# Seven block products for eight in the gate and up products of four feed-forward layers

## The chip, the core and the metric

The kernel runs on one core of a Trainium2 chip. The core has a matrix engine (TensorE, PE in the profile), VectorE (DVE), ScalarE (ACT), GpSimd (POOL) and SyncE (SP), which here only issues DMAs. Each engine takes its instructions in the order in which they stand in its own queue. The metric is the device time of one execution in microseconds (us); lower is better.

## The reference

Two blocks of two layers each run over 512 tokens of 1024 features in float32. Each layer has a mixer (windowed attention with sinks in A, neighbourhood attention on a grid in B, a gated delta rule in C, windowed attention with 16 meta tokens in D; A and B also attend to 256 memory tokens) and then a feed-forward (FFN) with 2816 hidden features:

```python
# A, B (first block)
h = rmsnorm(x, norm_ffn[i])
gu = h @ w_gate_up[i]
x = x + (jax.nn.silu(gu[..., :D_FF]) * gu[..., D_FF:]) @ w_down[i]
...
# C, D (second block): a causal convolution of 3 taps over the tokens of the gate
gate, val = jnp.split(h @ w_up, 2, -1)
gate = causal_dwconv(gate, conv_w)
return (jax.nn.silu(gate) * val) @ w_down
```

In the second block 16 meta tokens stand ahead of the 512, so that C's FFN has 528 tokens and D's needs 512 and a few before them for the convolution.

## The kernel before

Everything lies transposed: 128 features on the partitions, tokens along the free axis, so the stream is 8 tiles X[k] of 128 x 512 (or 528). Every float32 product is made of three matmuls (`mm3`): both operands are split into a high and a low part (`split`: ACT copies the high part, DVE subtracts it from the operand for the low part), and hi*hi, hi*lo and lo*hi are added in a PSUM bank.

`ffn` walks over NFF = 22 tiles f of 128 gate and 128 up columns. For each f two weight pieces of 4 K chunks x 256 columns (128 of the gate, 128 of the up half) are loaded by SP (`wcols`, `wpiece`: three `raw` buffers, four pairs `hi`, `lo`), split, and multiplied with the 8 operand tiles xs (`linT`): 8 x 3 matmuls for the gate and 24 for the up product, each over up to 512 tokens, which fill one PSUM bank. 528 tokens are taken as two halves of 264, in D the gate as 258 + 256. The norm's scale rs (one value per token) is not in the operands: it multiplies the products when they leave PSUM (`scaled`). At f = 0 it is still to come: `Held` keeps the products, `nj.sums()` and `nj.rows()` make rs, then they are scaled. In C and D `conv` follows on the gate (one ACT instruction and two on DVE), then SiLU on ACT (L877), the product with the up half (`ut`, L883) and its split into `ah`, `al`.

The down product runs over GROUPS of 8, 8 and 6 tiles f: after each group, for 8 output tiles j, 3 matmuls per f of the group are added in a bank (24, 24 and 18), from pieces of 256 output columns. The results of the first two groups are added to the stream X[j] on DVE (`resid`, L573). Those of the last go to `done`: a function of the next stage that adds the stream and starts the next norm, tile by tile, in A with a transposition of the token grid (`to_cols`, L1035), then the operands `xh`, `xl` of the next layer (L393, L394) and the sum of squares (L428).

A scheduler sets the order of the instructions on each engine from the order in which the code emits them, their priorities and the buffers that are free (62 `slot` buffers of 128 x 544, five `wk` buffers, three PSUM banks `mm`, others by the names `s` and `o`). During the FFN of A, `mid` calls steps of `load_biases`: six tiles `TB` of layer B's relative biases, by 96 small DMAs on GpSimd's queue. Layer B's memory keys and values, made in layer A, stay in slots until B uses them.

## Time and profile before

| | us |
|---|---|
| median of 3 runs | 2553.48 |
| lowest, highest | 2551.66, 2554.62 |
| span of the profiled execution | 2552.4 |
| PE busy | 2520.9 (99%) |
| DVE busy | 1423.0 (56%) |
| ACT busy | 968.8 (38%) |
| GpSimd busy | 275.8 (11%) |

The profiled execution took 2552.4 us from its first instruction to its last, 1.1 us under the median. The FFN of A lies at about 236 to 603 us of the span, B's at 800 to 1187, C's at 1576 to 1960 and D's at 2178 to the end. A matmul's recorded duration overlaps that of the next one, so its price in a stream is the distance between two starts. The granted clock is a share of TensorE's full speed.

### The profile page before, as it was taken

How to read it: one execution, taken by the hardware profiler on the slowest of the kernel's cores; microseconds unless marked ns; L12 is line 12 of the kernel's file. 1: busy time of each engine (PE TensorE's matmuls, PEld its weight loads, DVE VectorE, ACT ScalarE, POOL GpSimd, SP SyncE). 2: the span in 40 equal slices, each digit the busy share in tenths (PEclk: the TensorE clock that was granted, in tenths of full speed). 3: DMA queues.
4: the chain of work that ended last, by engine and by line, in shares of the span. 5: the costliest groups of instructions: out<-in, count | busy, mean ns of one | idle time of the engine just before them, and what ended most of it. 6: DMA issues, size and time to landing. Idle time of an engine off the chain costs nothing.

```text
span 2552.4 us, 40552 instructions
## 1 busy us (share of the span) xinstructions
PE 2520.9 (99%) x16222; PEld 2203.4 (86%) x16222; DVE 1423.0 (56%) x2838; ACT 968.8 (38%) x1687; POOL 275.8 (11%) x451
## 2 busy tenths in 40 slices
...
DMA packets 333648, 224.80 MB, mean 88 GB/s; under 512 B 43939, under 2 KB 324948, under 8 KB 333460
## 3 DMA queue, kind: packets, MB, share of 16 engines
...
## 4 chain that ended last, share of the span: by engine, by line
PE 47%; DVE 2%; issue 1%; POOL 0%; ACT 0%; POOLq 0%; DVEq 0%; ACTq 0%
PE mm L253 13%; PE mm L254 13%; PE mm L255 13%; PE pso L1874 1%; PE pss L1454 1%; PE pss L1447 1%; PE pss L1859 1%; PE pss L1431 0%; PE pss L339 0%; PE pss L733 0%; PE pss L1433 0%; PE pso L1879 0%; PE pss L734 0%; DVE xt L1420 0%; PE pss L1854 0%
## 5 line engine op out<-in xcount | busy, mean ns | idle before, releaser
L253 PE MATMUL mm<-xh,hi 128*128 128x264 f32 (+3 forms) x2752 | 916.4, 333 | 7.6 <-ACT xh L393 3.2
L254 PE MATMUL mm<-xl,hi 128*128 128x264 f32 (+3 forms) x2752 | 907.7, 330 | 0.5 <-DVE xl L394 0.5
L255 PE MATMUL mm<-xh,lo 128*128 128x264 f32 (+3 forms) x2752 | 906.1, 329 | 0.0
L217 DVE TENSOR_TENSOR lo<-raw,hi 128x1024 fp32r<-128x1024 f32 (+1 forms) x386 | 464.6, 1204 | 344.8 <-ACT hi L216 342.4
L216 ACT ACTIVATE hi<-raw 128x1024 fp32r<-128x1024 f32 (+1 forms) x386 | 400.2, 1039 | 660.6 <-PE mm L254 579.8
L253 PEld LDWEIGHTS mm<-xh,hi 128*128 128x128 f32 x2752 | 523.2, 190 | 61.7 <-issue 7.5
L254 PEld LDWEIGHTS mm<-xl,hi 128*128 128x128 f32 x2752 | 523.5, 190 | 47.2 <-DVE xl L394 1.3
L255 PEld LDWEIGHTS mm<-xh,lo 128*128 128x128 f32 x2752 | 523.3, 190 | 47.5 <-issue 0.5
L254 PE MATMUL mm<-al,hi 128*128 128x512 f32 (+1 forms) x880 | 308.0, 350 | 0.1
L253 PE MATMUL mm<-ah,hi 128*128 128x512 f32 (+1 forms) x880 | 308.0, 350 | 0.0
L255 PE MATMUL mm<-ah,lo 128*128 128x512 f32 (+1 forms) x880 | 307.8, 350 | 0.0
L573 DVE TENSOR_TENSOR xr<-mm,xr 128x264 f32<-128x264 f32 (+1 forms) x168 | 90.5, 542 | 188.0 <-PE mm L255 187.9
L254 PEld LDWEIGHTS mm<-al,hi 128*128 128x128 f32 x880 | 165.5, 188 | 23.1 <-DVE al L315 0.3
L253 PEld LDWEIGHTS mm<-ah,hi 128*128 128x128 f32 x880 | 165.6, 188 | 22.8
L255 PEld LDWEIGHTS mm<-ah,lo 128*128 128x128 f32 x880 | 165.4, 188 | 22.6
L290 DVE TENSOR_TENSOR gt<-mm,rs 128x512 f32<-128x512 f32 (+3 forms) x128 | 66.3, 518 | 185.5 <-PE mm L255 184.4
L877 ACT ACTIVATE gt<-gt 128x512 f32<-128x512 f32 x44 | 27.8, 632 | 176.6 <-DVE gt L290 176.4
L314 ACT ACTIVATE ah<-ut 128x512 fp32r<-128x512 f32 (+1 forms) x88 | 56.0, 636 | 86.3 <-DVE ut L883 86.3
L846 ACT ACTIVATE cy<-gt,fwcol 128x528 f32<-128x528 f32 (+1 forms) x44 | 32.1, 731 | 147.9 <-DVE gt L290 145.5
L254 PE MATMUL mm<-ol,hi 128*128 128x512 f32 (+1 forms) x256 | 87.6, 344 | 0.0
L255 PE MATMUL mm<-oh,lo 128*128 128x512 f32 (+1 forms) x256 | 87.4, 343 | 0.0
L290 DVE TENSOR_TENSOR ut<-mm,rs 128x512 f32<-128x512 f32 (+1 forms) x108 | 63.7, 590 | 42.2 <-PE mm L255 40.5
...
## 6 DMA issues: line engine op xcount, KB each, us to landing
raw<-in_w_gate_up_dram SPq DMA_DIRECT2D x176, 256.0 KB, 3.2
raw<-in_ffn_w_up_dram SPq DMA_DIRECT2D x176, 256.0 KB, 3.4
...
```

What stands on the lines that cost most here:

```text
L216: A.activation(r32(hi[:, :nk, :w]), raw[:, :nk, :w], AF.Copy)
L217: V.tensor_tensor(r32(lo[:, :nk, :w]), raw[:, :nk, :w], hi[:, :nk, :w], ALU.subtract)
L253: PE.matmul(ps, r32(hi), r32(xh), start=first, stop=False)
L254: PE.matmul(ps, r32(hi), r32(xl), start=False, stop=False)
L255: PE.matmul(ps, r32(lo), r32(xh), start=False, stop=last)
L290: V.tensor_tensor(dst[:, o:o + n], ps[:, :n], rs[:, o:o + n], ALU.mult)
L314: A.activation(r32(dst_h), src, AF.Copy)
L573: V.tensor_tensor(X[j][:, o:o + n], ps[:, :n], X[j][:, o:o + n], ALU.add)
L846: A.activation(out[:, lo:T], src[:, lo:T], AF.Copy, scale=taps[-1])
L877: A.activation(gt[:, w], gt[:, w], AF.Silu)
L1447: PE.matmul(py[q, h], am[q, h], x[q, h], start=True, stop=True)
L1454: PE.matmul(pzt[q, h], y[q, h], xt[q, h], start=True, stop=True)
```

## The change

For f >= NPLAIN = 3 the gate and up products of a tile are computed by blocks. The weights of f are a 2 x 2 array of blocks (first and second half of K, by gate and up columns), the normed operands another (halves of K by halves of the tokens), and the four results (gate and up by halves of the tokens) come from seven block products in place of eight, with sums of blocks ahead of and behind them. `seven` loads the two raw pieces, makes three new sums and one in place on DVE (L302 to L305) and splits seven blocks into four pieces `hi`, `lo`. `Blocks` builds the seven operands of the tokens for each of 4 K chunks: from `normed` (L995, DVE: x times the norm's weight times rs) with three subtractions on GpSimd (L339, L352, L357) and splits between them; this stands behind f = 0 and f = 1. `blocks_to` runs the seven products of 12 matmuls each in the order 1, 5, 6, 7, 2, 4, 3, over half the tokens (256 in A and B, 264 in C, 258 in D), three copies out of PSUM on ACT (L378, L380, L389), four additions on DVE (L383, L386, L392, L394) and one on GpSimd (L387). Products 2 and 3 go on adding to the banks of 1 and 5. Since the operands are normed, these tiles need no scaling by rs.

The down product has groups of 4, 4, 4, 4, 4 and 2 tiles. Its output tiles are emitted between the gate and up tiles of the next group, two after each f (four in the last group of two), and those of the last group at the end. `resid` runs for five groups. The biases `TB` go through a DRAM copy by 16 DMAs and 6 loads on SP's queue, and layer B's memory keys and values are written to DRAM and loaded back as `memb` there. Comments are gone, so lines move: L217 is L424 in the changed kernel, L290 is L398, L573 is L682, L883 is L1047, L1035 is L1200, L394 is L503, L428 is L537.

```diff
-GROUPS = [(0, 8), (8, 8), (16, 6)]
+GROUPS = [(0, 4), (4, 4), (8, 4), (12, 4), (16, 4), (20, 2)]
...
-NSLOT = 62
+NSLOT = 60
 NWK = 5
-NRAW = 3
+NRAW = 4
 NHI = 4
+NQT = 3
+NPLAIN = 3
...
-TAGS = {'t': (3, ['PT'])}
+TAGS = {'t': (3, ['PT', 's1', 's2', 's4'])}
...
+    def seven(loads, nk):
+        r0, r1 = [wp.tile([P, 4, 256], F32, tag="raw", name=nm("raw"), bufs=NRAW) for _ in range(2)]
+        for r, ld in zip((r0, r1), loads):
+            for n0, nn, src in ld:
+                nc.sync.dma_start(r[:, :nk, n0:n0 + nn], src)
...
+        V.tensor_tensor(s1, r0[b_], r1[b_], ALU.add)
+        V.tensor_tensor(s2, s1, r0[a_], ALU.subtract)
+        V.tensor_tensor(r0[b_], r0[a_], r0[b_], ALU.subtract)
+        V.tensor_tensor(s4, r1[a_], s2, ALU.subtract)
+        res = {}
+        for keys, srcs in (((1, 5), (r0[a_], s1)), ((6, 7), (s2, r0[b_])), ((2, 4), (r1[:, :nk, :],)), ((3,), (s4,))):
+            h, l = [wp.tile([P, 4, 256], F32, tag=x, name=nm(x), bufs=NHI) for x in ("hi", "lo")]
+            for i, src in enumerate(srcs):
+                w = slice(i * P, i * P + src.shape[2])
+                split(h[:, :nk, w], l[:, :nk, w], src)
+            for i, key in enumerate(keys):
+                res[key] = [(h[:, k, i * P:(i + 1) * P], l[:, k, i * P:(i + 1) * P]) for k in range(nk)]
+        return res
+    class Blocks:
+        def __init__(self, nk, o, n, tag, eng):
+            self.n, self.o, self.tag, self.eng = n, o, tag, eng
+            self.ops = {i: [None] * nk for i in range(1, 8)}
+            self.raw = [None] * nk
...
+        def first(self, k, z):
+            h, l = slot(self.tag), slot(self.tag)
+            v = self.win(z)
+            split(self.part(h, 0), self.part(l, 0), v[:, 0, :])
+            self.eng.tensor_tensor(v[:, 0, :], v[:, 1, :], v[:, 0, :], ALU.subtract)
+            split(self.part(h, 1), self.part(l, 1), v[:, 0, :])
+            for i, key in enumerate((1, 5)):
+                self.ops[key][k] = self.part(h, i), self.part(l, i)
+            self.raw[k] = v
+        def second(self, k, z):
+            v, t = self.win(z), self.raw[k]
+            h, l = slot(self.tag), slot(self.tag)
+            split(self.both(h), self.both(l), v)
+            for i, key in enumerate((2, 3)):
+                self.ops[key][k] = self.part(h, i), self.part(l, i)
+            self.eng.tensor_tensor(t, v[:, 1, :].unsqueeze(1).to_broadcast([P, 2, self.n]), t, ALU.subtract)
+            h, l = slot(self.tag), slot(self.tag)
+            split(self.both(h), self.both(l), t)
+            for i, key in enumerate((6, 7)):
+                self.ops[key][k] = self.part(h, i), self.part(l, i)
+            self.eng.tensor_tensor(v[:, 0, :], v[:, 0, :], t[:, 0, :], ALU.subtract)
+            h = slot(self.tag)
+            split(self.part(h, 0), self.part(h, 1), v[:, 0, :])
+            self.ops[4][k] = self.part(h, 0), self.part(h, 1)
+    def product(ps, i, ws, bl, more=False):
+        w, b = ws[i], bl.ops[i]
+        for k, ((hi, lo), (h, l)) in enumerate(zip(w, b)):
+            mm3(ps[:, :bl.n], hi, lo, h, l, not more and k == 0, k == len(w) - 1, more)
+    def blocks_to(ws, bl, c1, c2):
+        n = bl.n
+        (c11, c12), (c21, c22) = [[c[:, bl.o + i * n:bl.o + (i + 1) * n] for i in range(2)] for c in (c1, c2)]
+        pa, pd = mmps(), bank("s")
+        p1, u2 = [quarter("u")[:, :n] for _ in range(2)]
+        product(pa, 1, ws, bl)
+        A.copy(p1, pa[:, :n])
+        product(pd, 5, ws, bl)
+        A.copy(c22, pd[:, :n])
+        pb = bank("s")
+        product(pb, 6, ws, bl)
+        V.tensor_tensor(u2, pb[:, :n], p1, ALU.add)
+        pc = bank("o")
+        product(pc, 7, ws, bl)
+        V.tensor_tensor(c21, pc[:, :n], u2, ALU.add)
+        G.tensor_tensor(c22, c22, c21, ALU.add)
+        product(pa, 2, ws, bl, more=True)
+        A.copy(c11, pa[:, :n])
+        pe = mmps()
+        product(pe, 4, ws, bl)
+        V.tensor_tensor(c21, pe[:, :n], c21, ALU.add)
+        product(pd, 3, ws, bl, more=True)
+        V.tensor_tensor(c12, pd[:, :n], u2, ALU.add)
...
-                kst.append(stack_k(kt[t], NMEM, [(x[:, :256], x[:, 256:512]) for x in d]))
+                st = stack_k(kt[t], NMEM, [(x[:, :256], x[:, 256:512]) for x in d])
+                kst.append([(h, l, x) for (h, l), x in zip(st, d)])
...
+            if li:
+                d = dp.tile([5 * P, 512], F32, name="memd")
+                for i, t in enumerate([x for pair in kst for h in pair for x in [h[2]]] + [vs]):
+                    nc.sync.dma_start(d[i * P:(i + 1) * P, :], t[:, :512])
+                memK.append(d)
+                memV.append(None)
+                continue
             memK.append(kst)
             memV.append(vt)
+    def memory_back():
+        d = memK[1]
+        t = [slot("memb") for _ in range(5)]
+        for i, x in enumerate(t):
+            nc.sync.dma_start(x[:, :512], d[i * P:(i + 1) * P, :])
+        memK[1] = [[(t[2 * i + hh][:, :256], t[2 * i + hh][:, 256:512]) for hh in range(2)] for i in range(2)]
+        memV[1] = [t[4][:, :256], t[4][:, 256:512]]
...
     def ffn(X, T, nj, wgu, wd, taps, done, lo=0, mid=None):
         xs = nj.xs
         lg = max(0, lo - 2)
...
+        w = slice(lo, T)
+        lb = max(0, lo - 4)
+        xb = Blocks(4, lb, (T - lb) // 2, "xb", G)
+        def normed(k, rs):
+            z = wk("xn")
+            V.scalar_tensor_tensor(z[:, :T], X[k][:, :T], gcol(nj.key, k), rs[:, :T], ALU.mult, ALU.mult)
+            return z
+        state = {}
+        def up(f, put):
+            c = f * P
+            if mid is not None and f >= MID:
+                next(mid, None)
+            gt, ut = wk("gt"), wk("ut")
+            if f < NPLAIN:
                 pcs = [wcols(wgu, 4 * h, [(c, P), (DFF + c, P)]) for h in range(2)]
-                gt, ut = wk("gt"), wk("ut")
-                w = slice(lo, T)
                 if f == 0:
                     hg, hu = Held(gt), Held(ut)
                     run(linT(pcs, 0, xs, T, hg.take, lo=lg, wide=True))
                     nj.sums()
                     run(linT(pcs, 1, xs, T, hu.take, lo=lo))
-                    rs = nj.rows()
-                    hg.scale(rs)
+                    state["rs"] = nj.rows()
+                    hg.scale(state["rs"])
+                    hu.scale(state["rs"])
                 else:
-                    run(linT(pcs, 0, xs, T, lambda out: scaled(out, rs, gt), lo=lg))
-                if taps is not None:
-                    cy = wk("cy")
-                    conv(gt, taps(f), cy, T, lo)
-                    gt = cy
-                A.activation(gt[:, w], gt[:, w], AF.Silu)
-                if f == 0:
-                    hu.scale(rs)
-                else:
-                    run(linT(pcs, 1, xs, T, lambda out: scaled(out, rs, ut), lo=lo))
+                    run(linT(pcs, 0, xs, T, lambda out: scaled(out, state["rs"], gt), lo=lg))
+                    run(linT(pcs, 1, xs, T, lambda out: scaled(out, state["rs"], ut), lo=lo))
+            else:
+                ws = seven([kcols(wgu, 4 * h, 4, [(c, P), (DFF + c, P)]) for h in range(2)], 4)
+                blocks_to(ws, xb, gt, ut)
+            if taps is not None:
+                cy = wk("cy")
+                conv(gt, taps(f), cy, T, lo)
+                gt = cy
+            A.activation(gt[:, w], gt[:, w], AF.Silu)
+            put(gt, ut)
+            if f < 2:
+                for k in (2 * f, 2 * f + 1):
+                    xb.first(k, normed(k, state["rs"]))
+                    xb.second(k, normed(k + 4, state["rs"]))
+        def down(gi, acts):
+            f0, fn = GROUPS[gi]
+            for jp in range(4):
+                pcs = [wcols(wd, k0, [(jp * 256, 256)], min(4, f0 + fn - k0)) for k0 in range(f0, f0 + fn, 4)]
+                for t in range(2):
+                    fin = done if gi == len(GROUPS) - 1 else resid(X)
+                    run(linT(pcs, t, acts, T, lambda out, j=2 * jp + t: fin(j, out), fn, lo=lo, wide=jp + t == 0))
+                    yield
+        before = iter(())
+        for gi, (f0, fn) in enumerate(GROUPS):
+            acts = []
+            def put(gt, ut):
                 ah, al = slot("ah"), slot("al")
                 V.tensor_tensor(ut[:, w], ut[:, w], gt[:, w], ALU.mult)
                 split(ah[:, w], al[:, w], ut[:, w])
                 acts.append((ah, al))
-            for jp in range(4):
-                pcs = [wcols(wd, k0, [(jp * 256, 256)], min(4, f0 + fn - k0)) for k0 in range(f0, f0 + fn, 4)]
-                for t in range(2):
-                    j = 2 * jp + t
-                    fin = done if gi == len(GROUPS) - 1 else resid(X)
-                    run(linT(pcs, t, acts, T, lambda out, j=j, fin=fin: fin(j, out), fn, lo=lo, wide=j == 0))
+            for i in range(fn):
+                up(f0 + i, put)
+                for _ in range(8 * (i + 1) // fn - 8 * i // fn):
+                    next(before, None)
+            before = down(gi, acts)
+        run(before)
...
+        td = dp.tile([P, 6 * 512], F32, name="TBd")
+        for cc in range(16):
+            nc.sync.dma_start(td[8 * cc:8 * cc + 8, :].rearrange("p (i j) -> p i j", j=32),
+                              scap(15 - cc, [[4608, 8], [48, 96], [1, 32]]))
+            if cc > 1:
+                yield
         for hp in range(6):
-            t = slot("TB")
-            for cc in range(16):
-                G.dma_start(t[8 * cc:8 * cc + 8, :512].rearrange("p (i j) -> p i j", j=32),
-                            scap(hp * 768 + 15 - cc, [[4608, 8], [48, 16], [1, 32]]))
-            TB.append(t)
-            yield
+            TB.append(slot("TB"))
+            nc.sync.dma_start(TB[hp][:, :512], td[:, hp * 512:(hp + 1) * 512])
+        memory_back()
```

Three places show how the instructions stand. The first is DVE in the middle of layer A's FFN; before, two tiles f look like this (`gt` and `ut` are scaled products out of banks `mm`, `lo` low parts of weight pieces, `al` the low part of the activated tile):

```order
L315 TENSOR_TENSOR al_2724<-ut_2634,ah_2723 128x512
L217 TENSOR_TENSOR lo_2880<-raw_2876,hi_2879 128x1024
L290 TENSOR_TENSOR ut_2743<-mm_2771,rs_2711 128x512
L883 TENSOR_TENSOR ut_2743<-ut_2743,gt_2742 128x512
L217 TENSOR_TENSOR lo_2887<-raw_2883,hi_2886 128x1024
L315 TENSOR_TENSOR al_2798<-ut_2743,ah_2797 128x512
```

In the changed kernel, from the first PSUM addition of one tile (`u`) on, with the next tile's weight sums `s` and pieces `lo`, and the activated tile `ut` and its `al`:

```order
L383 TENSOR_TENSOR u_4047<-pss_4074,u_4046 128x256
L424 TENSOR_TENSOR lo_4152<-raw_4149,hi_4151 128x1024
L386 TENSOR_TENSOR ut_4010<-pso_4088,u_4047 128x256
L392 TENSOR_TENSOR ut_4010<-mm_4116,ut_4010 128x256
L424 TENSOR_TENSOR lo_4200<-raw_4186,hi_4199 128x4x128
L394 TENSOR_TENSOR gt_4009<-pss_4045,u_4047 128x256
L302 TENSOR_TENSOR s_4192<-raw_4186,raw_4187 128x512
L1047 TENSOR_TENSOR ut_4010<-ut_4010,gt_4009 128x512
L303 TENSOR_TENSOR s_4193<-s_4192,raw_4186 128x512
L304 TENSOR_TENSOR raw_4186<-raw_4186 128x4x128
L424 TENSOR_TENSOR al_4145<-ut_4010,ah_4144 128x512
L682 TENSOR_TENSOR xr_2343<-mm_4155,xr_2343 128x512
```

The low parts of the next tile's weights and of the down weights, and the next tile's sums, now stand between the four additions that empty the PSUM banks of this tile.

The second place is DVE at the start of layer A's FFN, where rs has just come; before:

```order
L290 TENSOR_TENSOR gt_2633<-mm_2635,rs_2711 128x512
L290 TENSOR_TENSOR ut_2634<-mm_2686,rs_2711 128x512
L883 TENSOR_TENSOR ut_2634<-ut_2634,gt_2633 128x512
L290 TENSOR_TENSOR gt_2742<-mm_2744,rs_2711 128x512
L315 TENSOR_TENSOR al_2724<-ut_2634,ah_2723 128x512
L217 TENSOR_TENSOR lo_2880<-raw_2876,hi_2879 128x1024
```

Now, with the normed tiles `xn` and the low parts `xb` of their blocks:

```order
L398 TENSOR_TENSOR gt_2625<-mm_2641,rs_2717 128x512
L398 TENSOR_TENSOR ut_2626<-mm_2692,rs_2717 128x512
L995 SCALAR_TENSOR_TENSOR xn_2734<-xr_2341,ncol,rs_2717 128x512
L995 SCALAR_TENSOR_TENSOR xn_2743<-xr_2345,ncol,rs_2717 128x512
L995 SCALAR_TENSOR_TENSOR xn_2758<-xr_2342,ncol,rs_2717 128x512
L1047 TENSOR_TENSOR ut_2626<-ut_2626,gt_2625 128x512
L995 SCALAR_TENSOR_TENSOR xn_2767<-xr_2346,ncol,rs_2717 128x512
L424 TENSOR_TENSOR al_2730<-ut_2626,ah_2729 128x512
L424 TENSOR_TENSOR xb_2737<-xn_2734,xb_2736 128x256
L398 TENSOR_TENSOR gt_2782<-mm_2798,rs_2717 128x512
L424 TENSOR_TENSOR xb_2746<-xn_2743,xb_2745 128x2x256
L424 TENSOR_TENSOR xb_2737<-xn_2734,xb_2736 128x256
```

Eight normed tiles and the low parts of the operands stand between the scaled products of the first three tiles.

The third place is PE at the end of layer A's FFN, where the output tiles of the last group follow one another in banks `mm` (`ah`, `al` are activated tiles, `hi`, `lo` parts of the down weights). Before, an output tile has 18 matmuls, of which the last ones and the first of the next tile are:

```order
L253 MATMUL mm_4920<-ah_4903,hi_4916 128x512
L254 MATMUL mm_4920<-al_4904,hi_4916 128x512
L255 MATMUL mm_4920<-ah_4903,lo_4917 128x512
L253 MATMUL mm_4941<-ah_4533,hi_4910 128x512
L254 MATMUL mm_4941<-al_4534,hi_4910 128x512
L255 MATMUL mm_4941<-ah_4533,lo_4911 128x512
L253 MATMUL mm_4941<-ah_4607,hi_4910 128x512
```

Now it has six, so that a whole output tile stands here with the ends of its neighbours:

```order
L253 MATMUL mm_6375<-ah_6296,hi_6371 128x512
L254 MATMUL mm_6375<-al_6297,hi_6371 128x512
L255 MATMUL mm_6375<-ah_6296,lo_6372 128x512
L253 MATMUL mm_6384<-ah_6088,hi_6371 128x512
L254 MATMUL mm_6384<-al_6089,hi_6371 128x512
L255 MATMUL mm_6384<-ah_6088,lo_6372 128x512
L253 MATMUL mm_6384<-ah_6296,hi_6371 128x512
L254 MATMUL mm_6384<-al_6297,hi_6371 128x512
L255 MATMUL mm_6384<-ah_6296,lo_6372 128x512
L253 MATMUL mm_6403<-ah_6088,hi_6399 128x512
```

The bank of an output tile closes after six matmuls where it closed after eighteen.

## Rows read from the trace of the kernel before

**Rows 1.** The page: busy time, share of the span and instructions of each engine.

```profile
PE 2520.9 (99%) x16222; PEld 2203.4 (86%) x16222; DVE 1423.0 (56%) x2838; ACT 968.8 (38%) x1687; POOL 275.8 (11%) x451
```

**Rows 2.** Windows: layer C's FFN; stretch, length, engines' busy us, clock, DMA share, GB/s.

```profile
1581.00:1960.00 379.00, 378.87 (x3116) 378.28 (x3115) 204.58 (x316) 122.34 (x151) 4.10 (x8) 1.00 0.32 94
```

**Rows 3.** Timeline of PE, FFNs of A, C, D: start us, us, instruction.

```profile
400.12 0.39 PE L255 MATMUL mm<-xh,lo 128*128 128x512 f32 x1
400.35 0.39 PE L253 MATMUL mm<-xh,hi 128*128 128x512 f32 x1
...
1699.93 0.29 PE L253 MATMUL mm<-ah,hi 128*128 128x264 f32 x1
1700.05 0.29 PE L254 MATMUL mm<-al,hi 128*128 128x264 f32 x1
...
2211.02 0.28 PE L255 MATMUL mm<-xh,lo 128*128 128x256 f32 x1
2211.14 0.28 PE L253 MATMUL mm<-xh,hi 128*128 128x256 f32 x1
```

**Rows 4.** SiLU (L877) in C and D: duration ns min/median/max, first and last start.

```profile
L877 ACT ACTIVATE cy<-cy x8: 644/646/648, 1725.4 to 1806.9; 128x528 f32<-128x528 f32 x8
...
L877 ACT ACTIVATE cy<-cy x8: 613/613/616, 2317.9 to 2396.5; 128x512 f32<-128x512 f32 x8
```

**Rows 5.** DVE groups by shape: line, tiles, count | busy us, mean ns.

```profile
L217 DVE TENSOR_TENSOR lo<-raw,hi 128x1024 fp32r<-128x1024 f32 x368 | 452.4, 1230 | 344.8 <-ACT hi L216 342.4 <-PE mm L284 2.0 <-DMA hwcol<-in_swa_q_norm_w_dram 0.2
...
L290 DVE TENSOR_TENSOR ut<-mm,rs 128x512 f32<-128x512 f32 x66 | 45.6, 692 | 40.5 <-PE mm L255 40.5
...
L849 DVE SCALAR_TENSOR_TENSOR cy<-gt,fwcol,cy 128x512 f32<-128x512 f32 x44 | 33.1, 752 | 17.9 <-ACT cy L846 17.2
...
L428 DVE TENSOR_TENSOR acc<-acc,sq 128x512 f32<-128x512 f32 x28 | 19.6, 701 | 0.8 <-ACT sq L418 0.4
...
L217 DVE TENSOR_TENSOR lo<-raw,hi 128x512 fp32r<-128x512 f32 x18 | 12.3, 683 | 0.0
...
L394 DVE SCALAR_TENSOR_TENSOR xl<-xr,ncol,xh 128x512 fp32r<-128x512 f32 x16 | 11.9, 748 | 3.7 <-ACT xh L393 3.7
...
L1035 DVE TENSOR_TENSOR xb<-mm,xr 128x512 f32<-128x512 f32 x8 | 9.3, 1169 | 2.6 <-PE mm L255 2.6
...
L290 DVE TENSOR_TENSOR gt<-mm,rs 128x256 f32<-128x256 f32 x21 | 8.9, 425 | 44.4 <-PE mm L255 44.4
```

**Rows 6.** Timeline of DVE at the start of the FFNs of A and C.

```profile
249.03 0.68 DVE L290 TENSOR_TENSOR gt<-mm,rs 128x512 f32<-128x512 f32 x1
249.64 0.68 DVE L290 TENSOR_TENSOR ut<-mm,rs 128x512 f32<-128x512 f32 x1
...
258.51 0.69 DVE L290 TENSOR_TENSOR ut<-mm,rs 128x512 f32<-128x512 f32 x1 [0.63 <-PE mm L255]
...
1589.58 0.70 DVE L311 TENSOR_TENSOR gt<-gt,rs 128x528 f32<-128x528 f32 x1
...
1600.55 0.43 DVE L290 TENSOR_TENSOR ut<-mm,rs 128x264 f32<-128x264 f32 x1
```

**Rows 7.** GpSimd group by shape: its sums of two tiles of 256 columns.

```profile
L1443 POOL TENSOR_TENSOR am<-ac,lev 128x256 f32<-128x256 f32 x20 | 17.1, 863 | 24.8 <-PE pss L1447 9.7 <-DVE yl L315 6.5 <-PE pss L1524 3.9
```

**Rows 8.** Windows in layer C: PE's busy time and the clock granted after it.

```profile
1187.00:1188.60 1.60, 0.30 (x3) 0.08 (x1) 1.60 (x3) 1.60 (x2) 1.60 (x1) 1.00 0.08 21
1188.60:1192.00 3.40, 3.28 (x16) 3.28 (x17) 3.21 (x6) 0.87 (x2) 3.40 (x12) 0.59 0.27 71
...
1280.00:1335.00 55.00, 55.00 (x387) 48.46 (x387) 20.59 (x35) 13.19 (x26) 6.78 (x12) 0.58 0.10 27
```

**Rows 9.** DMA issues: the gate and up weights, us from issue to landing.

```profile
raw<-in_w_gate_up_dram SPq DMA_DIRECT2D x176, 256.0 KB, 3.2
```

**Rows 10.** DVE groups from 1206 to 1222 us: the convolution's taps.

```profile
L849 DVE SCALAR_TENSOR_TENSOR qkv<-cg,cwcol,qkv 128x526 f32<-128x526 f32 x3 | 5.2, 1751 | 0.0
```

**Rows 11.** GpSimd groups from 1206 to 1222 us: its sums of two tiles.

```profile
L538 POOL TENSOR_TENSOR xc<-xc,r 128x512 f32<-128x512 f32 x8 | 12.9, 1644 | 8.9 <-ACT r L534 8.9
```

39 lines of the change are left out of this document (24 added, 15 removed).

## The prediction

> **What bounds the kernel now.** I read the totals of the page first: TensorE (PE) is busy 2520.9 of 2552.4 us, VectorE (DVE) 56%, ScalarE (ACT) 38% [rows 1]. Then the table of windows: in the feed-forward (FFN) of layer C PE is busy 378.87 of 379 us at granted clock 1.00, DVE 204.58, ACT 122.34, with a DMA share of 0.32 [rows 2]. So a FFN lasts as long as its matmuls, and a matmul's price is the distance from its start to the next, not its recorded duration: 0.23 us for 512 columns (400.12 to 400.35), 0.12 for 264 and 0.12 for 256 [rows 3]. Over many matmuls that is 0.231, 0.122 and 0.118, and the period of a tile f confirms it: the SiLU of f starts every 11.64 us in C (81.5 us over seven) and 11.23 in D (78.6 over seven) [rows 4], against 96 x 0.122 = 11.7 in C; A and B have 48 x 0.231 = 11.1.
>
> **What is removed.** For 19 of the 22 tiles of each FFN the gate and up products take seven block products of 4 K chunks x 3 matmuls = 84 matmuls of half the tokens, where 96 halves (or 48 wholes) stood. A and B: 84 x 0.118 = 9.91, so 1.18 less per tile; C: 84 x 0.122 = 10.25 against 11.71, 1.46 less; D (258 columns, 0.120): 10.08 against 11.23, 1.15 less. Times 19: 22.4 + 22.4 + 27.7 + 21.9 = **94.4 us**, if PE still never waits. The order of the changed program shows the 84, so the change does what it says. The down products cost PE the same whether in groups of 8 or of 4.
>
> Between 512 and 256 columns the trace shows 0.231 against 0.118 [rows 3], with as many weight loads as matmuls (3115 and 3116 [rows 2]): half the columns cost half, and the sum above stands on that. The page "TensorE: Matmul & The Clock Gate" of the Trainium skill, section "Back-to-back issue gap", gives 131 ns per matmul at 512 columns and 81 at 128 in a stream with weight loads. An estimate from its two figures, 106 ns at 256, would make a tile 84 x 0.106 = 8.9 us for 48 x 0.131 = 6.3, and the change a loss; the trace does not agree.
>
> **What DVE gets instead.** One period is now one f plus two down tiles. PE: 9.91 + 24 x 0.231 = 15.5 us (A, B); C 10.25 + 48 x 0.122 = 16.1; D 10.08 + 5.54 = 15.6. DVE in A, by [rows 5]: four weight sums of 512 elements, priced as other two-input SBUF sums (0.70), 2.8; the low parts of five half pieces (5 x 0.683) and one whole (1.23), 4.65; four additions out of PSUM (0.425), 1.7; gate times up and its low part, 1.4; the low part of the down weights 1.23; two residual additions 1.38. Sum **13.1 us** of 15.5. C and D add two convolution taps (0.75 each): about 15.0 of 16.1 and 14.6 of 15.6. Consecutive independent DVE instructions start about 0.08 us before the last one's recorded end (249.03 + 0.68 against the next at 249.64 [rows 6]), which gives back 1.5 to 1.8 per period. So DVE has 2 to 4 us left per period: it keeps up, but it goes from half to 85% busy, in order, and each PE bank and each weight piece waits for it. In the changed order low parts of the next tile's pieces stand ahead of additions that free banks. I charge 0.1 us per tile, 76 x 0.1 = **8 us** (ends: 0, and 0.86 per tile, as in rival 2). ACT, at a third of the window, gets no more than DVE does: nothing.
>
> **Start of each FFN.** The operands of the block products need the scale rs, so they can only be built between rs and tile f = 3. In A rs is used first at 249.03, f = 1 ends at 258.51, so f = 3 would start 11 us later, at 269.6: 20.6 us, plus 1 us until its last K chunk is wanted [rows 6]. DVE's work there, counted off the changed order: 8 normed tiles x 0.748 = 6.0; 6 scalings x 0.69 = 4.15; up times gate and low parts 3.4; low parts of weights (five halves, a whole) 4.64; the operands' low parts, 12 of 256 columns x 0.42 and 8 of 512 x 0.683 = 10.5. That is 28.7; the eight rows behind the last operand that the first product needs, 5.5, and 36 overlaps of 0.08 come off: 20.3. Each operand also goes GpSimd, ACT, DVE in turn; a GpSimd subtraction of 256 columns takes 0.86 [rows 7], and I charge 3 us of holes. 23.3 against 21.6: **2 us** of stall in A and in B. In C the room is 1589.58 to 1600.55 plus 11.7 = 22.7 plus 1 [rows 6], and DVE has six taps of 0.75 (4.5), and the scalings in halves (1.0 more) on top, with 5 us of holes since each tap waits for ACT: 20.3 + 5.5 + 5 = 30.8, so **7**; D, with the same taps and a room I take as C's, **7**. Sum 18 us. Ends: 0 if the holes are filled; 40 if GpSimd and DVE get in each other's way.
>
> **End of each FFN.** The last group has two tiles, so a down tile of it has 6 matmuls: 1.39 us, where it had 18 (4.16). Each of its eight outputs costs DVE in A the transposing addition 1.17, the operand's low part 0.75 and the norm's sum 0.70: 2.6 us, 21 for eight, plus three low parts of the next layer's weights (3.7), less 27 overlaps (2.2): 22.5 us [rows 5]. Until it needs the last operand, PE has 8 x 1.39 and 30 of the next layer's matmuls, 18 us; with 1.6 for the first tile, the stall is **6 us** in A. Before, the eight took PE 33 us and covered all of it. In B two norm sums are kept (0.70 more each, 5.6): **9.5** at the same addition. C adds in two halves (0.87): 2.3 per tile, 21.5 in all by the same count, against 8 x 1.46 and 7 of the next layer: **3**. D has no norm behind: 0. Sum 18.5; ends 5 and 35.
>
> **Clock.** After PE had run 0.30 of 1.6 us at 1187 the granted clock was 0.59 for the next 3.4 us, and the 55 us from 1280 ran at 0.58 [rows 8]: mostly the lower of the two levels (1.2 of 2.4 GHz). At the lower level 3.4 us of matmuls lose 1.7. Five stretches at the starts and ends that way: **8.5 us**.
>
> **Memory and queues.** 96 bias loads leave GpSimd's queue for 22 on SP's, and five tiles of layer B's memory keys and values go to DRAM and back, all on the queue of the weights. A 256 KB weight load lands 3.2 us after issue [rows 9] and now four raw buffers stand for three; the DMA share is a third. I take 0; one late piece in each direction would be 6.
>
> **Sum.** 2552.4 - 94.4 + 8 + 18 + 18.5 + 8.5 = 2511.0; the median stands 1.1 above the profiled span: **2512 us**.
>
> **Rivals.**
> 1. *The holes fill up.* DVE's sums of durations alone fit nearly everywhere; then half the start, half the tail and no slip or clock remain (18): 2552.4 - 94.4 + 18 + 1.1 = **2477**. For it: DVE at 13 to 15 of 15.5 to 16.1. Against: the tail's 22.5 against 18 needs no holes. 20%.
> 2. *The shared SBUF port.* While GpSimd runs two-input sums of 512 columns (1.64 us each), DVE's two-input taps take 1.75 us instead of 0.75 [rows 5, 10, 11]. The change puts a GpSimd addition into each of the 76 tiles, in reach of the two-input weight sums and low parts. The nearest price is GpSimd's own 256-column sum, 0.86 us. 76 x 0.86 = 65 us in place of the 8: **2569**, slower. It decides when the average tile loses more than 0.65 us (94.4 less 45 for starts, ends and clock, over 76) beyond PE's own time. For it: C and D have only 1 to 2 us to spare. Against: in A and B 2.4 to 4 us are free, more than one such wait. 13%. The Trainium skill, page "SBUF — State Buffer", section "Who interferes with whom", states that a DVE instruction with two SBUF inputs and a GpSimd instruction that reads SBUF exclude each other for the whole instruction; the stretched taps agree.
> 3. *Start and tail at their ends*, 40 and 35 for 36.5: **2551**, no change. 6%.
> 4. *The lower clock stays.* If three of the stalls bring the long stretch of layer C, 55 us at 0.58 [rows 8], which loses about 0.42 x 55 = 23 us each, 69 come on top: **2581**, slower. Against: FFN stretches are at 1.00 [rows 2]. 9%.
> 5. *Fixed cost per matmul:* if halving the columns saved a tenth less than the trace's 256-column rows say (0.130 for 0.118), 84 x 0.012 x 76 = 77 us: **2589**. The rows speak against it [rows 3]. 2%. The page's section on the issue gap, named above, points this way.
>
> **How the numbers follow.** Forecast 50% (2495 to 2535), rival 1 20%, rival 2 13%, 3 6%, 4 9%, 5 2%. A measurement of this kernel tells about 0.2% (5 us) from no change. Faster: 50 + 20, and 2 of rival 2, 2 of 3 and 1 of 4 where they strike mildly: 0.75. Same: 2 of rival 2, 4 of 3, 2 of 4: 0.08. Slower: 9 of 2, 6 of 4, 2 of 5: 0.17. The range, 2465 to 2565, leaves out the best end of rival 1 (4%), the far half of rival 2 (5%), rival 4 where it is slower (6%) and rival 5 (2%): 17%.
>
> **What would show it.** Right: FFN periods of about 15.5 us (f plus two down tiles) with PE unbroken, a stall of 2 to 8 us before the first matmuls of the fourth tile, and gaps after the last group's down tiles. Periods of 16.5 and more with DVE at 95% would be rival 2; no gap at f = 3, rival 1; granted clock under 0.9 in a FFN window, rival 4.

## The result and the profile after

The change takes 2524.49 us (median of four runs, 2523.07 to 2529.1) where the kernel before takes 2553.55; the ratio is 0.9885 with a 95% interval of 0.9868 to 0.9903. Run again beside the last experiment it gave 0.987 (0.9844 to 0.9896). So it is faster by 1.2%, 29 us, inside the range, with 12 us less gain than the forecast of 2512. The profiled execution spans 2521.3 us. Its totals, as in rows 1:

```profile
PE 2451.7 (97%) x17590; PEld 2222.2 (88%) x17590; DVE 1928.4 (76%) x3773; ACT 1212.4 (48%) x2299; POOL 358.6 (14%) x479
```

PE is busy 69 us less than in rows 1 and DVE 505 us more, but the span is only 31 us shorter: PE now waits.

In the middle of the feed-forwards (FFNs) it does not. The windows of B, C and D from the fourth or fifth block tile on, as in rows 2:

```profile
882.00:1100.00 218.00, 218.00 (x1520) 203.25 (x1519) 182.82 (x270) 102.41 (x170) 17.12 (x14) 1.00 0.36 106
...
1640.00:1900.00 260.00, 260.00 (x2132) 259.79 (x2131) 227.59 (x372) 125.98 (x207) 20.16 (x16) 1.00 0.34 100
...
2216.00:2460.00 244.00, 244.00 (x1673) 226.90 (x1672) 217.16 (x331) 122.82 (x204) 16.75 (x16) 1.00 0.36 104
```

PE is busy without a gap at granted clock 1.00, DVE (fifth column) for 84, 88 and 89% of the time. The SiLU (L1025 now, as in rows 4) gives the periods:

```profile
L1025 ACT ACTIVATE gt<-gt x14: 632/633/634, 894.3 to 1095.5; 128x512 f32<-128x512 f32 x14
```

```profile
L1025 ACT ACTIVATE cy<-cy x16: 631/632/635, 2223.2 to 2458.3; 128x512 f32<-128x512 f32 x16
```

```profile
L1025 ACT ACTIVATE cy<-cy x14: 644/646/648, 1649.9 to 1858.5; 128x528 f32<-128x528 f32 x14
```

Those are 201.2 / 13 = 15.48 us in B, 235.1 / 15 = 15.67 in D and 208.6 / 13 = 16.05 in C.

The gaps stand at both ends. PE at the first block tile of A, f = 3 (start, duration, instruction, idle before it):

```profile
270.51 0.28 PE L254 MATMUL mm<-xb,hi 128*128 128x256 f32 x1
270.63 0.28 PE L255 MATMUL mm<-xb,lo 128*128 128x256 f32 x1
274.81 0.38 PE L253 MATMUL mm<-xb,hi 128*128 128x256 f32 x1 [3.89 <-ACT xb L423]
275.87 0.39 PE L254 MATMUL mm<-xb,hi 128*128 128x256 f32 x1 [0.68 <-DVE xb L424]
```

Nine matmuls on the first three K chunks run, then PE waits 3.89 us for the operand of the fourth. In D there is one more wait, before any operand is wanted. DVE and PE there in f = 0:

```profile
2152.90 0.69 DVE L302 TENSOR_TENSOR s<-raw,raw 128x512 f32<-128x512 f32 x1 [5.29 <-DMA raw<-in_ffn_w_up_dram]
2153.51 0.70 DVE L537 TENSOR_TENSOR acc<-acc,sq 128x528 f32<-128x528 f32 x1
...
2154.36 1.25 PE L448 MATMUL pss<-ones_c,acc 128*128 128x1 f32 x10 [2.23 <-DVE acc L537]
...
2158.28 0.63 PE L254 MATMUL mm<-xl,hi 128*128 128x512 f32 x1
2158.71 0.63 PE L255 MATMUL mm<-xh,lo 128*128 128x512 f32 x1
```

The first weight sum of f = 3 (L302) stands in DVE's queue ahead of the norm's sum (L537) and waits for its weights to land. So PE waits 2.23 us for the norm's sum, and behind that gap its matmuls of 512 columns start 0.43 us apart in place of 0.231: the granted clock is 0.52 from 2157.0 to 2160.4 us. And at the end of A, between the output tiles of the last group:

```profile
588.08 0.40 PE L255 MATMUL mm<-ah,lo 128*128 128x512 f32 x1
589.62 0.47 PE L253 MATMUL mm<-ah,hi 128*128 128x512 f32 x1 [1.15 <-DVE xb L1200]
...
590.86 0.39 PE L255 MATMUL mm<-ah,lo 128*128 128x512 f32 x1
592.92 0.47 PE L253 MATMUL mm<-ah,hi 128*128 128x512 f32 x1 [1.68 <-DVE xb L1200]
```

After six matmuls PE waits until DVE's transposing addition (L1200, 1.15 us, which was L1035 with 1.17 in rows 5) has emptied a bank.

**How the kernels are compared below.** Totals of one kernel differ by up to 23 us from run to run, mostly with the granted clock in the mixers of layers C and D, which no edit here touches (C's took 369.7 to 388.3 us in the profiles). The same stretch of D's mixer in the changed kernel and in the run with the subtractions on VectorE:

```profile
1960.00:2140.00 180.00, 179.40 (x1464) 156.93 (x1463) 127.30 (x531) 106.91 (x261) 4.60 (x8) 0.98 0.24 60
```

```profile
1960.00:2140.00 180.00, 179.49 (x1421) 156.24 (x1420) 123.93 (x526) 102.33 (x253) 4.58 (x8) 0.94 0.22 57
```

At 0.98 that mixer took 210.7 us, at 0.94 it took 215.8. So each run is read by the time of its four FFNs, from the start of the first matmul of f = 0 to the start of the last matmul of the last output tile, and by PE's excess: the distances between the starts of its matmuls, less the usual distance for that many columns (0.231 us for 512, 0.122 for 264, 0.120 for 258, 0.118 for 256). Both come from the timeline of PE. In the kernel before, the four FFNs so counted start at 234.8, 819.9, 1573.9 and 2171.3 us (B's not at 800). The changed kernel's FFNs took 1463.5 us in its first profile and 1461.8 in its second, so differences under 2 us say nothing; the other kernels were profiled once each.

| four FFNs, us | A | B | C | D | sum | span |
|---|---|---|---|---|---|---|
| before | 367.1 | 365.7 | 387.6 | 375.0 | 1495.4 | 2552.4 |
| the change | 359.2 | 356.4 | 376.9 | 371.0 | 1463.5 | 2521.3 |
| the change, again | 359.2 | 356.3 | 376.1 | 370.2 | 1461.8 | 2521.9 |
| four plain tiles | 358.5 | 353.3 | 378.1 | 364.4 | 1454.3 | 2514.4 |
| five plain tiles | 353.3 | 350.1 | 377.0 | 363.4 | 1443.8 | 2488.9 |
| four plain tiles, operands spread | 357.0 | 353.9 | 373.1 | 361.5 | 1445.5 | 2501.6 |
| five plain tiles, operands spread | 354.3 | 351.2 | 374.1 | 359.8 | 1439.4 | 2503.0 |
| subtractions on VectorE | 357.1 | 353.9 | 374.7 | 368.1 | 1453.8 | 2518.0 |
| no added GpSimd work | 355.0 | 353.2 | 372.8 | 368.9 | 1449.9 | 2509.6 |
| last group of six | 355.7 | 353.5 | 375.3 | 370.8 | 1455.3 | 2515.5 |
| down groups alone | 371.7 | 370.0 | 389.8 | 374.6 | 1506.1 | 2566.2 |
| four, no GpSimd, six | 348.1 | 346.9 | 369.7 | 362.1 | 1426.8 | 2485.6 |
| five spread, no GpSimd, six | 350.3 | 347.3 | 364.5 | 356.6 | 1418.7 | 2468.9 |
| the same, four in A and B | 350.9 | 347.3 | 363.9 | 356.6 | 1418.7 | 2465.1 |

By PE alone the change would bring 1495.4 - 94.4 = 1401.0; it lost 62.5 of that. PE's excess over that of the kernel before says where: 10.9, 8.4, 14.4 and 17.7 us in f = 0 to 7 of A, B, C and D, together 51; 3.5, 3.6, 1.7 and 0 behind f = 21, together 8.8, and 2.6 more at the start of layer B; 2 to 3 in the middle. Of the 51, some 12 us are the lower clock behind the gaps: matmuls that followed one another without a gap, but further apart, while the granted clock was 0.5 (9 us in the second profile). In D 3.6 of the 17.7 lie in f = 0, where the norm's sum waits. The outside of the FFNs as a whole, the start of layer B with it, is 1 us longer.

### The profile page after: what moved, and what is told of

Its sections match the earlier page's. It is cut to its first block, busy times and chain, and to the rows that moved or that the text cites. A ratio compares the mean times of both kernels' runs of the same rounds, so it can differ in the third digit from the quotient of the medians.

```text
span 2521.3 us, 45248 instructions
## 1 busy us (share of the span) xinstructions
PE 2451.7 (97%) x17590; PEld 2222.2 (88%) x17590; DVE 1928.4 (76%) x3773; ACT 1212.4 (48%) x2299; POOL 358.6 (14%) x479
## 4 chain that ended last, share of the span: by engine, by line
PE 62%; DVE 7%; issue 2%; ACT 1%; POOL 1%; DMA 0%; SPq 0%; POOLq 0%; DVEq 0%; ACTq 0%
PE mm L253 13%; PE mm L254 13%; PE mm L255 13%; PE pss L255 3%; PE pss L254 3%; PE pss L253 3%; DVE lo L424 1%; PE pso L255 1%; PE pso L253 1%; PE pso L254 1%; DVE xb L424 1%; PE pso L803 1%; PE pso L2043 1%; PE pss L1616 1%; PE pss L842 1%
## 5 line engine op out<-in xcount | busy, mean ns | idle before, releaser
L424 DVE TENSOR_TENSOR lo<-raw,hi 128x1024 fp32r<-128x1024 f32 (+1 forms) x462 | 487.8, 1058 | 116.8 <-ACT hi L423 111.5
L253 PE MATMUL mm<-xh,hi 128*128 128x264 f32 (+3 forms) x1080 | 360.7, 335 | 9.9 <-DVE xc L1379 2.7
L254 PE MATMUL mm<-xl,hi 128*128 128x264 f32 (+3 forms) x1080 | 352.0, 326 | 0.3 <-DVE xl L503 0.3
L255 PE MATMUL mm<-xh,lo 128*128 128x264 f32 (+3 forms) x1080 | 351.0, 325 | 0.0
L253 PE MATMUL mm<-xb,hi 128*128 128x256 f32 (+2 forms) x912 | 260.5, 286 | 10.1 <-ACT xb L423 7.7
L253 PE MATMUL pss<-xb,hi 128*128 128x256 f32 (+2 forms) x912 | 260.0, 285 | 7.2 <-ACT xb L423 5.6
L255 PE MATMUL mm<-xb,lo 128*128 128x256 f32 (+2 forms) x912 | 259.5, 285 | 4.3 <-DVE lo L424 4.0
L254 PE MATMUL pss<-xb,hi 128*128 128x256 f32 (+2 forms) x912 | 259.7, 285 | 1.5 <-DVE xb L424 1.5
L254 PE MATMUL mm<-xb,hi 128*128 128x256 f32 (+2 forms) x912 | 259.0, 284 | 1.4 <-DVE xb L424 1.4
L255 PE MATMUL pss<-xb,lo 128*128 128x256 f32 (+2 forms) x912 | 258.8, 284 | 0.0
L253 PEld LDWEIGHTS mm<-xh,hi 128*128 128x128 f32 x1080 | 210.1, 195 | 33.1 <-issue 7.4
L387 POOL TENSOR_TENSOR ut<-ut 128x256 f32<-128x256 f32 (+2 forms) x76 | 82.8, 1089 | 1064.0 <-ACT hi L423 681.2
L254 PEld LDWEIGHTS mm<-xl,hi 128*128 128x128 f32 x1080 | 209.8, 194 | 14.8 <-DVE xl L503 1.5
L255 PEld LDWEIGHTS mm<-xh,lo 128*128 128x128 f32 x1080 | 209.8, 194 | 14.4 <-issue 0.5
L682 DVE TENSOR_TENSOR xr<-mm,xr 128x512 f32<-128x512 f32 (+1 forms) x288 | 159.5, 557 | 74.0 <-PE mm L255 73.5
L424 DVE TENSOR_TENSOR lo<-s,hi 128x512 fp32r<-128x512 f32 x228 | 183.2, 808 | 4.4 <-ACT hi L423 0.4
```

Of the source, the lines that this page charges most:

```text
L253: PE.matmul(ps, r32(hi), r32(xh), start=first, stop=False, skip_group_check=more)
L254: PE.matmul(ps, r32(hi), r32(xl), start=False, stop=False, skip_group_check=more)
L255: PE.matmul(ps, r32(lo), r32(xh), start=False, stop=last, skip_group_check=more)
L387: G.tensor_tensor(c22, c22, c21, ALU.add)
L424: V.tensor_tensor(r32(dst_l), src, dst_h, ALU.subtract)
L682: V.tensor_tensor(X[j][:, o:o + n], ps[:, :n], X[j][:, o:o + n], ALU.add)
```

## Experiments

The theory to be tested: VectorE (DVE) is too full between the norm's scale rs and the first block tiles, and the short last group leaves it no cover at the end. The rivals: the chain through GpSimd with its blocking of DVE's port makes the operands late; the place of the work in DVE's queue, and not its amount, decides; the ends belong to the norm and not to the group's length.

### One more plain tile

```diff
-NPLAIN = 3
+NPLAIN = 4
```

> One more tile per feed-forward (f = 3) is computed plainly, so the operands of the block products have one more tile of time (11.1 to 11.7 us) to be built. The change lost 7.9, 7.9, 12.2 and 12.9 us of PE in the stretch behind the start of f = 3 in A, B, C and D (excess of the matmuls' distances over their usual 0.118 to 0.231 us). Theory 'room' (the operands come too late because too little time lies between the norm's scale and f = 3): nearly all of the 41 us goes, the plain tile costs 1.18 + 1.18 + 1.46 + 1.15 = 5 us, so about 2490 to 2495 against 2524.5. Rival 'work' (VectorE is simply full there, a plain tile brings it some 5 us more): about half goes, 2505 to 2512. Rival 'order' (where the operands stand in the queue sets the wait, wherever the first block product is): the gaps move to f = 4, 2528 to 2532.

Measured: 0.9833 of before (0.9786 to 0.9881), FFNs 1454.3 us. That is 9.2 us better, or 14 before the plain tile's 5 us: nearest to 'work', and short of it. In A and B the wait for the operands at the first block tile is gone, but smaller ones for the low parts of weights stand a tile later (PE is idle for 0.67, 0.77 and 2.45 us in A, 1.10, 0.77 and 1.19 in B), and in C PE now waits 6.5 us inside f = 2. The norm's sum in D's f = 0 no longer waits: that excess, 1.9 to 3.9 us in the five profiles with three plain tiles and block products, is nothing in every run with four or five, so a part of the 9.2 has nothing to do with the operands.

### The operands' subtractions on VectorE

```diff
-        xb = Blocks(4, lb, (T - lb) // 2, "xb", G)
+        xb = Blocks(4, lb, (T - lb) // 2, "xb", V)
```

> The 12 subtractions per feed-forward that build the operands are done by VectorE and not by GpSimd. In the changed kernel a GpSimd subtraction of 256 columns took 0.75 us alone and 1.78 us at 268.8 us beside VectorE's two-input work, and VectorE's low parts of 512 columns took 1.31 and 1.22 instead of 0.68 beside GpSimd. Theory 'port and hand-over' (the chain VectorE, GpSimd, ACT, VectorE with mutual blocking makes the operands late): the gaps behind f = 3 shrink by a third to a half, 2504 to 2515. Rival 'VectorE full': 4 x (2 x 0.42 + 0.69) = 6.1 us more work per feed-forward on VectorE, all on the path: 2540 to 2550.

Measured: 0.9825 (0.9777 to 0.9873), 2515.85 us, FFNs 1453.8 us, 9.7 less. 'VectorE full' is out; it is nearest to 'port and hand-over', whose range it just misses: the excess in f = 0 to 7 fell by about 9 us of 51, less than a third. DVE has 12 instructions more per feed-forward and is done earlier. The groups of DVE by shape from 249 to 290 us (count, busy us, mean ns), of the changed kernel:

```profile
L424 DVE TENSOR_TENSOR xb<-xn,xb 128x512 fp32r<-128x512 f32 x8 | 6.9, 868 | 0.2 <-ACT xb L423 0.2
L995 DVE SCALAR_TENSOR_TENSOR xn<-xr,ncol,rs 128x512 f32<-128x512 f32 x8 | 6.8, 875 | 0.0
...
L424 DVE TENSOR_TENSOR lo<-s,hi 128x512 fp32r<-128x512 f32 x5 | 4.6, 928 | 0.0
```

and with the subtractions on VectorE:

```profile
L995 DVE SCALAR_TENSOR_TENSOR xn<-xr,ncol,rs 128x512 f32<-128x512 f32 x8 | 5.8, 744 | 0.0
L424 DVE TENSOR_TENSOR xb<-xn,xb 128x512 fp32r<-128x512 f32 x8 | 5.5, 681 | 0.0
...
L424 DVE TENSOR_TENSOR lo<-s,hi 128x512 fp32r<-128x512 f32 x6 | 4.0, 681 | 0.0
```

Beside GpSimd the same three kinds took 8 x 0.187 + 8 x 0.131 + 5 x 0.247 = 3.8 us more, and with the low parts of raw weights (four at 967 for 681 ns, two at 1763 for 1217) 6.0. The subtractions themselves cost DVE 4 x (0.684 + 2 x 0.42) = 6.1. So GpSimd saved DVE next to nothing there, and its longer chain came on top. GpSimd's side in A in the changed kernel, its first subtraction and those at f = 3:

```profile
254.88 0.75 POOL L339 TENSOR_TENSOR xn<-xn 128x256 f32<-128x256 f32 x1 [88.32 <-DVE xb L424]
...
268.82 1.78 POOL L339 TENSOR_TENSOR xn<-xn 128x256 f32<-128x256 f32 x1 [2.59 <-DVE xb L424]
271.59 1.27 POOL L352 TENSOR_TENSOR xn<-xn,xn 128x512 f32<-128x512 f32 x1 [0.99 <-DVE xb L424]
```

The same subtraction took 0.75 us at 254.88 and 1.78 at 268.82, beside DVE's two-input instructions, and the operand for which PE waits 3.89 us stands behind it in ACT's queue.

### The down groups alone

```diff
-NPLAIN = 3
+NPLAIN = 22
...
-            if f < 2:
+            if f < 2 and NPLAIN < NFF:
```

Here no tile is computed by block products.

> All 22 tiles are computed plainly and no operands for block products are built; the groups of 4, 4, 4, 4, 4, 2 tiles with the down tiles between the gate and up tiles, the 60 slots and the queues stay as in the change. So this is the second part of the change alone, against the kernel before (2553.5). Theory: the short last group costs about 4 us in A, 5 in B, 2 in C as in the change, the rest nothing: 2560 to 2567. Rival 'grouping costs nothing, the ends belong to the block products': 2552 to 2556. Rival 'the interleaving itself is what gains': below 2548.

Measured: 1.0072 (1.0048 to 1.0096), slower; FFNs 1506.1 us, 10.7 more than before, and 3.1 more in layer B ahead of its FFN. The excess is 3.4, 3.4 and 1.7 us behind f = 21 of A, B and C, as in the change, and next to nothing elsewhere (1.7 in A's f = 3 to 7). The second part of the change alone costs some 14 us by the profiles; it gains nothing by itself. What the block products would take with the old groups was not run.

### A last group of six

```diff
-GROUPS = [(0, 4), (4, 4), (8, 4), (12, 4), (16, 4), (20, 2)]
+GROUPS = [(0, 4), (4, 4), (8, 4), (12, 4), (16, 6)]
```

> The last group has 6 tiles (f = 16 to 21) as in the kernel before, so that an output tile at the end has 18 matmuls again (4.2 us) for VectorE's 2.6 us; the groups are 4, 4, 4, 4, 6. Theory 'short last group': the gaps at the ends go (4.3 us in A, some 5 to 8 in B with the start of the next layer, 2 in C): 2509 to 2516. Rival 'the ends are set by the norm's chain, not by the length of the outputs': 2521 to 2527. Rival 'slots': six activated tiles and four of the group ahead hold 20 of the 60 slots at once, and PE waits in the middle: over 2530.

Measured: 0.9838 (0.9788 to 0.9888), FFNs 1455.3 us, 8.2 less, and layer B up to its FFN 218.7 for 221.2. The last stretches of A and B, by the windows of this run:

```profile
553.00:592.00 39.00, 39.00 (x170) 31.76 (x170) 26.89 (x33) 17.73 (x25) 7.97 (x24) 1.00 0.53 167
1126.00:1164.00 38.00, 38.00 (x165) 30.52 (x163) 30.11 (x44) 21.60 (x44) 13.62 (x10) 1.00 0.35 97
```

PE has no gap left, and the slots are not short. So the ends belong to the group's length.

### No added GpSimd work at all

```diff
-        xb = Blocks(4, lb, (T - lb) // 2, "xb", G)
+        xb = Blocks(4, lb, (T - lb) // 2, "xb", V)
...
-        G.tensor_tensor(c22, c22, c21, ALU.add)
+        V.tensor_tensor(c22, c22, c21, ALU.add)
```

> Both kinds of added GpSimd work go to VectorE: the 12 subtractions per feed-forward that build the operands, and the addition of each of the 76 tiles (L387). The four feed-forwards took 1463.5 us from their first matmul to their last in the changed kernel and 1453.8 with the subtractions alone moved. Theory 'the port is paid only at the start': between the tiles VectorE has room, so the additions of the 76 tiles cost nothing wherever they stand; 1449 to 1455. Rival 'the port is paid in every tile': PE's excess in the middle of the feed-forwards (0.2, 0.5, 0 and 1.7 us) and behind the start falls further, under 1446. Rival 'VectorE full': 0.43 us more per tile shows, over 1460.

Measured: 0.9821 (0.9777 to 0.9866), FFNs 1449.9 us: 3.9 less than with the subtractions alone moved, inside what the first theory gave. PE's excess from f = 8 on stays as it was; the 3.9 lie in f = 0 to 7. Yet the port is paid throughout the tiles of the change. GpSimd's addition there and the low parts of the weight sums, all of the kernel:

```profile
L387 POOL TENSOR_TENSOR ut<-ut 128x256 f32<-128x256 f32 x38 | 40.7, 1072 | 521.1 <-ACT hi L423 284.4 <-DVE ut L386 236.7
```

```profile
L424 DVE TENSOR_TENSOR lo<-s,hi 128x512 fp32r<-128x512 f32 x228 | 183.2, 808 | 4.4 <-ACT hi L423 0.4
```

and those low parts in this run:

```profile
L424 DVE TENSOR_TENSOR lo<-s,hi 128x512 fp32r<-128x512 f32 x228 | 155.1, 684 | 6.9 <-ACT hi L423 5.3
```

On these alone DVE lost 28 us in the change; in the middle it fell into DVE's free time.

### Number and place of the operand work

The number of plain tiles and the place of the operands were changed apart and together: five plain tiles with the operands where they were, four with the four K chunks behind f = 0, 1, 1 and 2, and five with one chunk behind each of f = 0 to 3.

```diff
-NPLAIN = 3
+NPLAIN = 5
```

> Five plain tiles, but the operands of two K chunks behind f = 0 and two behind f = 1 as in the change, so that against the run with one chunk behind each of four tiles (1439.4 us for the four feed-forwards) only the place of the operands differs, and against the one with four plain tiles (1454.3) only their number. Theory 'number of plain tiles': 1436 to 1443, as with one chunk per tile. Theory 'place': VectorE's queue is still blocked by 23 us of operand work in f = 1 and f = 2, so PE still waits there: 1450 to 1460.

Measured: FFNs 1443.8 us, 0.8 above the range of 'number' and far from 'place' (one run, no interval).

```diff
-NPLAIN = 3
+NPLAIN = 4
...
-            if f < 2:
-                for k in (2 * f, 2 * f + 1):
+            if f < 3:
+                for k in ((0,), (1, 2), (3,))[f]:
```

> Four plain tiles, and the four K chunks of operands behind f = 0 (one), f = 1 (two) and f = 2 (one); subtractions on GpSimd. Against the run with four plain tiles (1454.3 us for the four feed-forwards, 13.3 and 8.2 us of it PE's excess before f = 3 in C and D over the kernel before) only the place differs. Theory 'place': that excess goes and what comes behind is no larger, 1438 to 1448. Theory 'number': 1451 to 1457.

Measured: FFNs 1445.5 us, within what 'place' gave (one run). But the excess in C and D did not go as expected: in f = 0 to 7 it was 14.1 and 10.3 us with four tiles and the operands where they were, and is 9.5 and 7.2 here.

```diff
-NPLAIN = 3
+NPLAIN = 5
...
-            if f < 2:
-                for k in (2 * f, 2 * f + 1):
+            if f < 4:
+                for k in (f,):
```

> Five tiles (f = 0 to 4) are computed plainly, and the operands of the block products are built one K chunk behind each of f = 0 to 3, not two behind f = 0 and f = 1; subtractions stay on GpSimd. Theory 'work' (VectorE is full from the norm's scale to some tiles after f = 3; it needs plain tiles, each of which leaves it about 6 us, to get through 23 us of operand work): the 50 us that PE lost in f = 0 to 7 of the four feed-forwards fall to 5 to 15, the two plain tiles cost 10: the four take 1425 to 1440 us in place of 1463.5. Rival 'hand-over' (GpSimd's chain is what is late): the gaps follow the last operand to f = 5, 1460 to 1470.

Measured: 0.977 (0.9745 to 0.9796), FFNs 1439.4 us, at the far edge of 'work'.

So the number gives 9.2 us for the fourth tile and 10.5 for the fifth, net of what they cost PE; spreading gives 8.8 with four and 4.4 with five. Both rivals hold in part. The place is seen with five plain tiles in C, where DVE's queue in f = 2 reads:

```profile
1570.35 0.42 DVE L424 TENSOR_TENSOR xb<-xn,xb 128x264 fp32r<-128x264 f32 x1
1570.69 0.76 DVE L995 SCALAR_TENSOR_TENSOR xn<-xr,ncol,rs 128x528 f32<-128x528 f32 x1
1571.37 0.70 DVE L424 TENSOR_TENSOR xb<-xn,xb 128x528 fp32r<-128x528 f32 x1
1573.16 0.43 DVE L424 TENSOR_TENSOR xb<-xn,xb 128x264 fp32r<-128x264 f32 x1 [1.08 <-ACT xb L423]
1573.51 0.77 DVE L398 TENSOR_TENSOR gt<-mm,rs 128x264 f32<-128x264 f32 x2
```

The scaled gate `gt` (L398), which frees the banks that PE's next products need, stands behind operands that wait for ACT. PE had started its last matmul at 1567.34 and went on 6.5 us later than usual. Operand work that is not urgent yet stands ahead of a scaling that is.

### All together

The versions with four plain tiles (operands where they were) and with five (spread) take over the last group of six and have no GpSimd work; these are the edits above, joined.

> Four plain tiles, no GpSimd work, and a last group of six tiles together. Alone these brought the four feed-forwards from 1463.5 us to 1454.3, 1453.8 and 1455.3. If they add up: 1434 to 1438, and 2.5 us less at the start of layer B. If the first two take away the same gaps, about 1445.

Measured: 0.9711 (0.9666 to 0.9756), FFNs 1426.8 us, under both expectations: the gain is more than the sum of the single gains (1463.5 - 9.2 - 9.7 - 8.2 = 1436.4; with the additions off GpSimd 1432.5).

> Five plain tiles with one K chunk of operands behind each of the first four, no GpSimd work, and a last group of six. By the theory 'work' PE loses next to nothing at the start and at the end, and the four feed-forwards take 1401 (PE alone, 19 tiles by seven products) + 10 (two more plain tiles) + 5 to 10: 1416 to 1421 us, some 2475 in all, against 1495.4 in the kernel before. If VectorE is still full at the start: 1430 to 1440.

Measured: 0.9694 (0.9663 to 0.9725), 2482.0 us median, FFNs 1418.7 us, as the theory had it; the total is 7 us above the 2475 named, inside the spread of its runs (2470.64 to 2484.41). The start of the FFNs of A, C and D, first in the changed kernel and then in this one:

```profile
234.00:320.00 86.00, 80.66 (x475) 71.02 (x474) 77.05 (x125) 42.57 (x74) 23.22 (x25) 0.98 0.36 97
1556.00:1626.00 70.00, 62.05 (x460) 59.86 (x459) 61.55 (x107) 34.26 (x63) 15.81 (x14) 0.93 0.19 55
2150.00:2222.00 72.00, 62.54 (x371) 55.39 (x370) 63.91 (x108) 36.30 (x65) 15.04 (x14) 0.91 0.19 55
```

```profile
234.00:320.00 86.00, 86.00 (x454) 73.48 (x453) 69.01 (x121) 39.38 (x64) 5.38 (x10) 1.00 0.38 102
1530.00:1600.00 70.00, 69.92 (x572) 69.55 (x572) 61.37 (x118) 34.23 (x60) 0.00 (x0) 1.00 0.22 66
2108.00:2180.00 72.00, 71.44 (x461) 64.25 (x461) 62.69 (x117) 36.09 (x61) 0.00 (x0) 1.00 0.27 81
```

PE's gaps are all but gone in these stretches and the lower clock is gone from the FFNs; what is left of A's excess, 2.8 us, lies behind 329 us.

The last edit keeps five plain tiles for C and D and takes four in A and B, and ran beside the changed kernel:

```diff
+        plain = 4 if taps is None else 5
+        spread = {0: (0,), 1: (1, 2), 2: (3,)} if taps is None else {0: (0,), 1: (1,), 2: (2,), 3: (3,)}
...
-            if f < NPLAIN:
+            if f < plain:
...
-            if f < 4:
-                for k in (f,):
+            if f in spread:
+                for k in spread[f]:
```

> The changed kernel once more, on the chip of the next run, as its measure. 2512 to 2530 us; the four feed-forwards 1463 us as in its first profile, give or take 2; where the total differs from 2521.3 it is in the mixers of layers C and D, where the granted clock was 0.94 to 0.98 from run to run.

Measured: 2522.77 us, FFNs 1461.8.

> As the version with five plain tiles, no GpSimd work and a last group of six, but A and B (no convolution on VectorE) with four plain tiles and the four K chunks of operands behind f = 0, 1, 1 and 2. Theory 'work': A and B keep 2 to 4 us less VectorE work per tile than C and D, so four plain tiles are enough there; each saves 1.2 us: the four feed-forwards 1414 to 1418 us against 1418.7 with five. Rival: A and B's gaps grow by more than the 1.2 us: over 1420.

Measured: 0.9686 (0.9657 to 0.9715), FFNs 1418.7 us, between the two expectations: A's excess in f = 3 to 7 rose from 3.2 to 5.2 and B's from 0.3 to 1.4, together about as much as the two plain tiles cost PE. It is the same as five tiles everywhere. Both beat the change: 3.1% under the kernel before, where the change has 1.2 to 1.3.

## Why the prediction was right, and where it was not

- **The price of a matmul**: right. Periods of 15.48 us in B, 16.05 in C and 15.67 in D were forecast as 15.5, 16.1 and 15.6. Half the columns cost half, so the gain of 94.4 us was there to be had, and rival 5 is out.
- **DVE beside PE in the middle**: right, 84 to 89% busy where 85% was forecast. The 8 us for slips were 2 to 3.
- **The start of each FFN: the step that failed.** It was put at 18 us (2, 2, 7, 7). The excess there was 51 (10.9, 8.4, 14.4, 17.7), some 40 without the lower clock, which the prediction counts apart: more than double, at its far end. Four things were left out. The work was counted at the durations of the kernel before, and beside GpSimd it took 6 us more in A (the run with the subtractions moved). The account closed with the operands of the first product, but DVE stayed full behind them: with four plain tiles PE waited in A for the low parts of weights instead. In C and D the operands stand in DVE's queue ahead of the scaling that frees PE's banks in f = 2, so that PE waited before the first block tile (the run with five plain tiles). And in D a weight sum of f = 3 stood ahead of the norm's sum and waited for its weights, 3.6 us in f = 0 with the clock behind it. 23.3 against 21.6 us was a margin of the size of what had been rounded off. In A, 2.8 of the 10.9 us lie at 330 to 350 us, where bias loads stand on SP's queue. For the most part they are not the operands' doing: 1.7 us stand there with no block product at all. They point to the bias loads, since B, which has none, and the kernel before, which has them on GpSimd's queue, lose nothing there; no run tried it.
- **The end of each FFN**: the mechanism was right, the size too large: 18.5 us forecast, 12 seen, of which the last group of six took away 10.7. A's 6 were 3.5 and, at the start of layer B, 2.6. B's 9.5 were 3.6 and, at the start of C, 2.5 over the first hundred matmuls, of which 0.7 was left after 220; C's 3 were 1.7. What was wrong in B, where a second norm sum was counted as 5.6 us more on the path, was not tried; the 9.5 does not follow from its own terms either, since 6 and 5.6 make 11.6.
- **Clock**: about right, 8.5 us set apart and some 12 and 9 seen in the two profiles. The granted clock fell at the starts, behind the gaps. Two windows of the changed kernel in C:

```profile
1596.00:1600.00 4.00, 0.88 (x3) 0.70 (x3) 2.90 (x7) 0.42 (x1) 2.21 (x2) 0.64 0.00 0
1600.00:1604.00 4.00, 4.00 (x20) 4.00 (x20) 3.58 (x7) 2.53 (x5) 2.58 (x3) 0.51 0.28 96
```

  After 0.88 busy us of 4, PE ran 4 us at the lower level (1.2 of 2.4 GHz). In the version without waits it is gone.
- **Memory and queues**: put at nothing, and nothing showed but the weight load that D's f = 0 waited for and what A's 2.8 us may hold.
- **Sum**: losses of 53 us were forecast, 62.5 came in the FFNs and 1 outside. A start too small by about 22 and a clock too small by 1 to 3 stood against an end and slips too large by about 12. That the total came within 12 us is in part the luck of errors that cancel.
- **A slip in the arithmetic**: the 106 ns at 256 columns is the mean of the two figures that the prediction takes from the Trainium skill (page "TensorE: Matmul & The Clock Gate", section "Back-to-back issue gap"). An estimate for 256 columns on a straight line between them is 98 ns. It makes the change a loss too, and the trace, at 118 ns against 231 for 512 columns, agrees with neither.
- **The rivals.** Rival 2, the port, is real but works at another place: taking the additions of the 76 tiles off GpSimd gave 3.9 us, all of it in f = 0 to 7, far from the 0.65 per tile from which it decides; at the start moving the subtractions gave 9.7. The Trainium skill's rule (page "SBUF — State Buffer", section "Who interferes with whom"), that a DVE instruction with two SBUF inputs contends with a GpSimd instruction that reads SBUF, agrees with both sides of the trace: DVE's low part 868 for 681 ns, GpSimd's subtraction 1.78 for 0.75 us. Rival 3 had the start's end right (40) and the tail's wrong (35, it was 12). Rivals 1 and 4 did not come: the gaps stayed, and the lower clock did not last.
